# High and low tokens as one 512-column matmul in the feed-forward input projections and the second merge

## The chip, the cores and the metric

One NeuronCore of a Trainium2 chip runs the whole program. The metric is device time in microseconds, as the median of the runs; lower is better. Engines are called PE (TensorE, matmuls), ACT (ScalarE), DVE (VectorE), POOL (GpSimd) and SP (SyncE, which issues most of the transfers).

## What is computed

256 tokens with 2048 channels pass through four blocks of layers, all in float32. Two attention layers come first (one with a learned choice of keys), then a block with two mixers (sparse attention and a gated delta rule), whose outputs are merged by sigmoid gates, then a feed-forward part and a last norm. Cut to what the change touches, the reference is:

```
g_nsa, g_dn = split(sigmoid(merge_g), 2)          # merge_g: 4096 of the columns of h @ w_in
mixed = g_nsa * (o_nsa @ w_up_nsa) + g_dn * (o_dn @ w_up_dn)
x  = x + mixed @ w_o
h2 = rms_norm(x, norm2_w)
x  = x + (silu(h2 @ w_ffn_gate) * (h2 @ w_ffn_up)) @ w_ffn_down     # 2048 -> 5632 -> 2048
return rms_norm(x, norm_f_w)
```

## The kernel before

Every large product goes through one function, `gemm` (L121). Activations stay in SBUF, weights stream through once. To keep float32 precision with one-pass matmuls, both operands are split into a high part (the value rounded to the matmul's format) and a low part (the rest), and a product is the sum of three: high x high, high x low, low x high.

*Activations.* `new_T` (L206) makes a pair of tiles `hi` and `lo`, each [128 channels, 4 chunks, 256 tokens], for 512 channels. A product over 2048 channels takes a list of four such pairs, one over 1024 (`w_up_dn`) two. `to_T` and `x_T` (L211, L238) fill a pair from transposes on PE; ACT writes `hi`, DVE writes `lo`. The pairs have two tags of eight buffers, which other split tiles share (`slot`, L51).

*Weights.* For 512 input channels (loop `g`) SP loads a tile `raw` of 1 MB, [128, 4 chunks, 512 columns] (L134), into one of three buffers. Each half of it is cast on ACT to `wh` (L139) and subtracted on DVE to `wl` (L140); both have three buffers. A `wh`/`wl` pair of [128, 2, 512] so feeds two chunks.

*Matmuls.* `gemm` has two forms. In the token-major one (L152 to L157) the activations are loaded into the array and 512 columns of weights stream past them. In the channel-major one (`flip=True`, L145 to L150) 128 columns of weights are loaded and the 256 tokens stream past: first `hi` by `wh`, then `lo` by `wh`, then `hi` by `wl`, all added into one 256-column half of a PSUM bank. The result is 512 channels in two banks, and `evac(b, psum)` is called for both at the end. There are four banks for products (tag `mm`), so the next product fills the other two.

*Around the change.* In `second` (L1213 to L1302), after all mixers, a loop over four blocks of 512 channels computes the second merge: a gate product over 2048 channels (L1285, evacuated by `mgate`, L1264: DVE multiplies by the row of the norm's factors, ACT takes the tanh), then the product with `w_up_dn` (L1297), whose `evac` (L1287) multiplies by the gate, adds the first merge's block `md` and splits the sum into `mT`. Four token-major products with `w_o` follow (L1301); after each, one block of the new residual is normed and transposed into the list `h2`. In `ffn` (L1313) the 11 blocks of 512 hidden channels come in parts of 4, 4 and 3. For each block there is a gate product (L1329, `evac_g`: DVE multiplies by the row, ACT takes the silu) and an up product (L1338, `evac_u`: DVE multiplies by the row and by the gate, then the block is split). After each part the token-major products with `w_ffn_down` follow (L1348). Before the loop `row_of` (L166) turns the norm's factors into a row on all partitions by two small matmuls (L175) and a copy (L176).

*What sets the order.* Each engine runs its instructions in program order and waits on semaphores. The framework orders the traced instructions by a model of their times when the program is built, so the order on each engine is fixed before the run. Small background tasks are traced between the matmuls by `tick` (L92).

Of the kernel before, what the change touches and what calls it, by code (L numbers as in the profile page):

```python
# [11 lines left out]
F32 = mybir.dt.float32  # L12
# [14 lines left out]
class Kern:  # L27
    """The whole forward pass; activations stay in SBUF, weights stream through once."""

    def __init__(self, ctx, tc, d, out, stop=None):  # L30
# [9 lines left out]
        self.flip = False  # L40
        self.finished = set()

# [32 lines left out]
    def defer(self, n, fn):  # L75
        """trace fn after n further ticks"""
        self.later.append([n, fn])
# [14 lines left out]
    def tick(self):  # L92
        """advance deferred work and the background chains"""
# [27 lines left out]
    def gemm(self, xT, W, c0, n, evac, ng=4, split=False, flip=False):  # L121
# [3 lines left out]
        pt = [self.ps.tile([P, 512], F32, tag="mm", bufs=4, name="mm") for _ in range(2)]  # L125
        for g in range(ng):
# [8 lines left out]
            hi, lo = xT[g]  # L135
            for h in range(2):
                wh = self.sb.tile([P, 2, n], F32R, tag="wh", bufs=3, name="wh")
                wl = self.sb.tile([P, 2, n], F32R, tag="wl", bufs=3, name="wl")
                nc.scalar.copy(wh, raw[:, 2 * h:2 * h + 2])  # L139
                nc.vector.tensor_tensor(wl, raw[:, 2 * h:2 * h + 2], wh.bitcast(F32), ALU.subtract)  # L140
# [20 lines left out]

    @staticmethod
    def c2(ap):
        return ap.rearrange("p (c n) -> p c n", c=2)

    def row_of(self, r):  # L166
        """per-token columns r[t] [128, 1] -> [128, 2 (broadcast), 256 tokens] on every partition"""
# [11 lines left out]
    def gemm_by_tile(self, xT, W, c0, n, evac, ng):  # L179
        """a narrow gemm that keeps its split weights and ends one token tile before the other"""  # L180
        nc = self.nc
        ws = []
        for g in range(ng):
# [3 lines left out]
            for h in range(2):  # L187
# [4 lines left out]
                ws.append((wh, wl))  # L192
        for t in range(2):
            o = self.ps.tile([P, 512], F32, tag="mm", bufs=4, name="mm")[:, :n]
            ts = slice(t * P, (t + 1) * P)
            for g in range(ng):
                hi, lo = xT[g]
# [8 lines left out]
    def new_T(self):  # L206
        hi = self.sb.tile([P, 4, T], F32R, tag="hi", bufs=8, name="hi")
        lo = self.sb.tile([P, 4, T], F32R, tag="lo", bufs=8, name="lo")
        return hi, lo

    def to_T(self, src, gain=None, scale=None):  # L211
        """src(t, c): [128 tokens, 128 channels]; returns the split transpose of 4 chunks."""
        nc = self.nc
        hi, lo = self.new_T()
# [21 lines left out]
        return hi, lo  # L236
# [7 lines left out]
    def rsq(self, out, in_, mul, n, eps=EPS):  # L244
        """out = (in_ * mul + eps) ** -0.5"""
# [8 lines left out]
    def norm_rstd(self, ss, dst=None):  # L254
        """ss: per token tile [128, 4] block sums of squares -> (rstd, rstd / 2, rstd^2 / 128)"""
# [11 lines left out]
    def rope4(self, o, x, tC, tS, scal=None, heads=4, hd=128):  # L267
        """o = x * C + swap(x) * S over [128, heads, hd]; x in PSUM or SBUF; scal per partition."""
# [20 lines left out]
    def trans4(self, src, dst, scale=None, n=4, eng=None):  # L289
        """dst [128, n*128] = per-128-column-chunk transposes of src [128, n*128]."""  # L290
# [36 lines left out]
    def park_x(self):  # L327
        """the residual waits in DRAM while the mixers need its room"""
# [22 lines left out]
    def gains2(self):  # L351
        """per-channel columns of the second block: conv taps, position embeddings, norm gain"""
# [15 lines left out]
    def tables(self, rope, qn, kn, wait=0):  # L368
        """rope tables with a per-dimension gain folded in: [128, t, (C | S)]"""
# [28 lines left out]
    def attn_qprep(self, t, ps, tabs, r, r2, st):  # L398
        """raw q block of 4 heads in PSUM -> roped (gain in), transposed; st: scale per head."""
# [15 lines left out]
    def pipeline(self, units, stages):  # L415
        """software pipeline: one stage of each unit in flight per step"""
# [104 lines left out]
    def split_into(self, hi, lo, cs, a):  # L521
        """chunks cs of a split transpose from a [128, len(cs), 256]"""
# [3 lines left out]
    def residual_block(self, j, gain, ss, hT, last=False):  # L526
        """evacuation of block j of a projection onto the residual, then the next input's block"""
# [981 lines left out]
```

## Time and profile before

| | |
|---|---|
| runs | 2310.85, 2311.62, 2311.79 us; median 2311.62 |
| span of the profiled execution | 2308.8 us; the profile gives no other time of this execution |
| PE, loads of weights into PE | busy 2295.5 us (99%), 2094.7 us (91%) |
| DVE, ACT, POOL | busy 1395.8 us (60%), 1089.4 us (47%), 133.6 us (6%) |
| data moved by DMA | 404.70 MB, mean 175 GB/s |
| second merge ends, w_o ends | at about 1455 and 1547 us of the span; the feed-forward part follows |

The time of a run counts from the outside; the span is from the first to the last instruction of one execution under the profiler. Busy time is the union of an engine's instructions. Matmuls overlap on PE: a row's length is not the distance to the next start, and that distance has to be read from starts and counts. An idle time is put down to the instruction that released the semaphore.

### The profile page before, as it was taken

How to read it: one execution, taken by the hardware profiler on the slowest of the kernel's cores; microseconds unless marked ns; L12 is line 12 of the kernel's file. 1: busy time of each engine (PE TensorE's matmuls, PEld its weight loads, DVE VectorE, ACT ScalarE, POOL GpSimd, SP SyncE). 2: the span in 40 equal slices, each digit the busy share in tenths (PEclk: the TensorE clock that was granted, in tenths of full speed). 3: DMA queues.
4: the chain of work that ended last, by engine and by line, in shares of the span. 5: the costliest groups of instructions: out<-in, count | busy, mean ns of one | idle time of the engine just before them, and what ended most of it. 6: DMA issues, size and time to landing. Idle time of an engine off the chain costs nothing.

```text
span 2308.8 us, 39431 instructions
## 1 busy us (share of the span) xinstructions
PE 2295.5 (99%) x16446; PEld 2094.7 (91%) x16446; DVE 1395.8 (60%) x2073; ACT 1089.4 (47%) x1758; POOL 133.6 (6%) x233
## 2 busy tenths in 40 slices
PE   9999999999999999999999999999999999999998
PEld 8878998888998888999999999889998899989997
DVE  5686765656665656878675655555555455554555
ACT  5555644456544434564534444454443344433444
POOL 1011100112100300011101000000000000000000
PEclk9999999999999999999999999999999999999999
DMA  7544455654556754344443665555555555555554
GB/s 230 193 149 153 140 183 182 189 176 137 167 183 208 240 157 152 112 164 130 146 148 120 205 225 183 182 192 191 183 183 189 192 184 183 183 182 184 182 185 143
DMA packets 209811, 404.70 MB, mean 175 GB/s; under 512 B 7376, under 2 KB 25776, under 8 KB 209632
## 3 DMA queue, kind: packets, MB, share of 16 engines
q1 hardware_dynamic: 206880, 394.04, 52.5%
q0 software_dynamic: 2752, 8.13, 1.2%
q8 instruction: 129, 2.11, 0.4%
q14 instruction: 50, 0.41, 0.1%
HBM read 397.95 MB, written 4.19 MB: 174 GB/s over the span
## 4 chain that ended last, share of the span: by engine, by line
PE 99%; DMA 0%; DVE 0%; SPq 0%; ACT 0%; issue 0%; ACTq 0%; POOLq 0%; POOL 0%
PE mm L150 16%; PE mm L148 16%; PE mm L149 16%; PE mm L157 14%; PE mm L156 14%; PE mm L155 14%; PE lg L440 1%; PE tr L294 1%; PE tp L219 1%; PE hid L994 1%; PE nl L1086 0%; PE pt L473 0%; PE ib L638 0%; DMA x<-in_x_dram 0%; PE ov L490 0%; PE ov L491 0%
## 5 line engine op out<-in xcount | busy, mean ns | idle before, releaser
L140 DVE TENSOR_TENSOR wl<-raw,wh 128x1024 fp32r<-128x1024 f32 (+4 forms) x760 | 902.6, 1188 | 794.2 <-ACT wh L139 793.1
L139 ACT CAST wh<-raw 128x1024 fp32r<-128x1024 f32 (+4 forms) x760 | 775.9, 1021 | 1028.5 <-PE mm L149 550.3
L150 PE MATMUL mm<-hi,wl 128*128 128x256 f32 x3072 | 868.9, 284 | 0.0
L148 PE MATMUL mm<-hi,wh 128*128 128x256 f32 x3072 | 868.4, 283 | 0.0
L149 PE MATMUL mm<-lo,wh 128*128 128x256 f32 x3072 | 868.1, 283 | 0.0
L148 PEld LDWEIGHTS mm<-hi,wh 128*128 128x128 f32 x3072 | 579.8, 189 | 1.5 <-issue 0.5
L149 PEld LDWEIGHTS mm<-lo,wh 128*128 128x128 f32 x3072 | 579.2, 189 | 0.8 <-issue 0.2
L150 PEld LDWEIGHTS mm<-hi,wl 128*128 128x128 f32 x3072 | 577.9, 188 | 1.0 <-issue 0.2
L156 PE MATMUL mm<-wl,hi 128*128 128x512 f32 (+4 forms) x1504 | 574.6, 383 | 0.2 <-DVE wl L140 0.2
L157 PE MATMUL mm<-wh,lo 128*128 128x512 f32 (+4 forms) x1504 | 570.6, 381 | 0.0
L155 PE MATMUL mm<-wh,hi 128*128 128x512 f32 (+4 forms) x1504 | 529.3, 382 | 0.0
L156 PEld LDWEIGHTS mm<-wl,hi 128*128 128x128 f32 x1504 | 283.3, 188 | 55.4 <-issue 0.6
L157 PEld LDWEIGHTS mm<-wh,lo 128*128 128x128 f32 x1504 | 283.1, 188 | 55.0 <-issue 1.5
L155 PEld LDWEIGHTS mm<-wh,hi 128*128 128x128 f32 x1504 | 281.1, 189 | 56.2 <-issue 1.3
L248 POOL TENSOR_SCALAR rsqv<-nsum 128x1 f32<-128x1 f32 x10 | 3.5, 351 | 1228.4 <-DVE nsum L1361 744.4
L233 ACT ACTIVATE hi<-tp,gT 128x256 fp32r<-128x256 f32 x64 | 27.6, 471 | 21.3 <-PE tp L219 18.9
L454 ACT ACTIVATE lg<-lg,nb 128x128 f32<-128x128 f32 (+1 forms) x64 | 28.4, 445 | 16.7 <-POOL nb L447 16.7
L234 DVE SCALAR_TENSOR_TENSOR lo<-tp,gT,hi 128x256 fp32r<-128x256 f32 x64 | 28.4, 478 | 12.4 <-ACT hi L233 12.0
L730 DVE SCALAR_TENSOR_TENSOR cv<-raw,cols,cv 128x255 f32<-128x255 f32 (+2 forms) x72 | 31.1, 475 | 1.8 <-ACT cv L727 1.7
L252 ACT ACTIVATE junk<-x 128x512 bf16<-128x512 f32 (+1 forms) x42 | 25.6, 610 | 6.0 <-DMA x<-in_x_dram 2.2
L252 ACT ACTIVATE junk<-mm 128x128 bf16<-128x128 f32 x80 | 22.2, 278 | 7.3 <-PE mm L157 5.8
L440 PE MATMUL lg<-kT,qT 128*128 128x256 f32 (+1 forms) x128 | 23.7, 327 | 0.0
(378 smaller groups left out, 1386.2 us busy)
## 6 DMA issues: line engine op xcount, KB each, us to landing
raw<-in_w_in_dram SPq DMA_DIRECT2D x76, 1024.0 KB, 5.1
raw<-in_w_ffn_gate_dram SPq DMA_DIRECT2D x44, 1024.0 KB, 5.2
raw<-in_w_ffn_up_dram SPq DMA_DIRECT2D x44, 1024.0 KB, 5.2
raw<-in_w_ffn_down_dram SPq DMA_DIRECT2D x41, 1024.0 KB, 5.1
raw<-in_a_w_in_dram SPq DMA_DIRECT2D x40, 1024.0 KB, 5.1
raw<-in_b_w_in_dram SPq DMA_DIRECT2D x40, 1024.0 KB, 5.1
raw<-in_a_w_out_dram SPq DMA_DIRECT2D x16, 1024.0 KB, 5.0
raw<-in_b_w_out_dram SPq DMA_DIRECT2D x16, 1024.0 KB, 5.1
```

The source lines that it names most:

```text
L139: nc.scalar.copy(wh, raw[:, 2 * h:2 * h + 2])
L140: nc.vector.tensor_tensor(wl, raw[:, 2 * h:2 * h + 2], wh.bitcast(F32), ALU.subtract)
L148: nc.tensor.matmul(o, wh[:, c, ms], hi[:, kc], start=first and m % 2 == 0, stop=False)
L149: nc.tensor.matmul(o, wh[:, c, ms], lo[:, kc], start=False, stop=False)
L150: nc.tensor.matmul(o, wl[:, c, ms], hi[:, kc], start=False, stop=last and m % 2 == 1)
L155: nc.tensor.matmul(o, xh, wh[:, c], start=first, stop=False)
L156: nc.tensor.matmul(o, xh, wl[:, c], start=False, stop=False)
L157: nc.tensor.matmul(o, xl, wh[:, c], start=False, stop=last)
L234: nc.vector.scalar_tensor_tensor(lo[:, k], tp[:, c], g, hi[:, k].bitcast(F32), ALU.mult, ALU.subtract)
L252: self.nc.scalar.activation(self.junk()[:, :w], in_, AF.Square, accum_out=accum)
L440: nc.tensor.matmul(lb[:, i * S:(i + 1) * S], qT[:, h * P:(h + 1) * P], kT[:, :S], start=True, stop=True)
L730: v.scalar_tensor_tensor(o[:, s:], x[:, :T - s], self.convw[:, k:k + 1], o[:, s:], ALU.mult, ALU.add)
```

## The change

Two kinds of products get a function of their own, `gemm_T`: the gate and up products of the feed-forward part, and both products of the second merge. The first merge, the attention layers' gates and the delta rule's inputs keep `gemm` with `flip=True`.

In `gemm_T` the outer loop runs over two halves of 256 output channels. A half takes two banks, one for each 128 channels. `raw` is [128, 8 chunks, 256 columns]: 1 MB as before, over 1024 input channels, in rows of 1 KB. A `wh`/`wl` pair is [128, 4, 256] and feeds four chunks. For each chunk and each 128 channels there are two matmuls: `wh` with the 512 columns of high and low tokens side by side, into the whole bank, and `wl` with the 256 high ones into the bank's first half. The high and low tokens therefore share a tile, [128, 4, 2, 256], with one tag `hl` of eight buffers of double size. The evacuation runs after each half: `add_halves` copies the second half of a bank out on ACT and adds the first on DVE, and only then come the row and the rest; in `w_up_dn`'s evacuation the sum goes through a tile `halves` that has one buffer. Since the first `raw` covers 1024 channels, a product's start asks for two blocks of its input list.

The core of the diff:

```diff
     def slot(self, name, dt=F32):
-        self.flip = not self.flip
-        return self.sb.tile([P, 2, 512], dt, tag="hi" if self.flip else "lo", bufs=8, name=name)
+        if self.half is not None:
+            b, self.half = self.half, None
+        else:
+            t = self.sb.tile([P, 2, 2, 512], F32, tag="hl", bufs=8, name="half")
+            b, self.half = t[:, 0], t[:, 1]
+        return b if dt is F32 else b.bitcast(dt)
...
+    def weights(self, raw, h, n):
+        nc = self.nc
+        k = raw.shape[1] // 2
+        wh = self.sb.tile([P, k, n], F32R, tag="wh", bufs=3, name="wh")
+        wl = self.sb.tile([P, k, n], F32R, tag="wl", bufs=3, name="wl")
+        nc.scalar.copy(wh, raw[:, k * h:k * h + k])
+        nc.vector.tensor_tensor(wl, raw[:, k * h:k * h + k], wh.bitcast(F32), ALU.subtract)
+        return wh, wl
...
+    def gemm_T(self, xT, W, c0, evac, ng=4):
+        nc = self.nc
+        for b in range(2):
+            pt = self.banks()
+            for g2 in range(ng // 2):
+                self.flush(lambda: len(xT) > 2 * g2 + 1 and None not in xT[2 * g2:2 * g2 + 2])
+                raw = self.sb.tile([P, 8, T], F32, tag="raw", bufs=3, name="raw")
+                nc.sync.dma_start(raw, W[g2 * 1024:(g2 + 1) * 1024,
+                                         c0 + b * T:c0 + (b + 1) * T].rearrange("(c p) n -> p c n", p=P))
+                for h in range(2):
+                    wh, wl = self.weights(raw, h, T)
+                    hl = xT[2 * g2 + h][2]
+                    for c in range(4):
+                        first = g2 == 0 and h == 0 and c == 0
+                        last = g2 == ng // 2 - 1 and h == 1 and c == 3
+                        for m in range(2):
+                            ms = slice(m * P, (m + 1) * P)
+                            nc.tensor.matmul(self.c2(pt[m]), wh[:, c, ms], hl[:, c],
+                                             start=first, stop=False)
+                            nc.tensor.matmul(pt[m][:, :T], wl[:, c, ms], hl[:, c, 0],
+                                             start=False, stop=last)
+                        if c % 2:
+                            self.tick()
+            evac(b, pt)
...
+    def add_halves(self, o, bank):
+        self.nc.scalar.copy(o, bank[:, T:])
+        self.nc.vector.tensor_tensor(o, bank[:, :T], o, ALU.add)
+
+    def joined(self, o, pt, row):
+        for i in range(2):
+            self.add_halves(o[:, i], pt[i])
+        self.nc.vector.tensor_tensor(o, o, row, ALU.mult)
...
     def new_T(self):
-        hi = self.sb.tile([P, 4, T], F32R, tag="hi", bufs=8, name="hi")
-        lo = self.sb.tile([P, 4, T], F32R, tag="lo", bufs=8, name="lo")
-        return hi, lo
+        hl = self.sb.tile([P, 4, 2, T], F32R, tag="hl", bufs=8, name="hl")
+        return hl[:, :, 0], hl[:, :, 1], hl
...
-            self.gemm(hT, W, 6696 + 2048 + 512 * j, 512, lambda b, ps: mgate(m[b], ps), flip=True)
+            self.gemm_T(hT, W, 6696 + 2048 + 512 * j, lambda b, pt: mgate_T(m[b], pt))
...
-                v.scalar_tensor_tensor(m[b], m[b], 1.0, ps, ALU.add, ALU.mult)
+                for i in range(2):
+                    up, mi = self.halves(), m[b][:, i]
+                    self.add_halves(up, pt[i])
+                    v.scalar_tensor_tensor(mi, mi, 1.0, up, ALU.add, ALU.mult)
...
-            self.gemm(dT, d["w_up_dn_2"][0], 512 * j, 512, evac, ng=2, flip=True)
+            self.gemm_T(dT, d["w_up_dn_2"][0], 512 * j, evac, ng=2)
...
-                    v.tensor_tensor(s[b], ps, row, ALU.mult)
+                    self.joined(s[b], pt, row)
...
-                self.gemm(h2, d["w_ffn_gate_2"][0], 512 * jb, 512, evac_g, flip=True)
+                self.gemm_T(h2, d["w_ffn_gate_2"][0], 512 * jb, evac_g)
...
-                self.gemm(h2, d["w_ffn_up_2"][0], 512 * jb, 512, evac_u, flip=True)
+                self.gemm_T(h2, d["w_ffn_up_2"][0], 512 * jb, evac_u)
```

Two places show how the instructions are laid out now. The first is PE where one product of the feed-forward part ends and the next begins; `mm` is a bank, `hi`, `lo` and `hl` are split activations, and the number after a name tells buffers apart. Before:

```order
L148 MATMUL mm_16376<-hi_15603,wh_16407 128x256
L149 MATMUL mm_16376<-lo_15604,wh_16407 128x256
L150 MATMUL mm_16376<-hi_15603,wl_16408 128x256
L148 MATMUL mm_16375<-hi_15767,wh_16437 128x256
L149 MATMUL mm_16375<-lo_15768,wh_16437 128x256
L150 MATMUL mm_16375<-hi_15767,wl_16438 128x256
```

With the change, where a half of a product ends and the next begins:

```order
L196 MATMUL mm_15892<-hl_15804,wh_15957 128x512
L198 MATMUL mm_15892<-hl_15804,wl_15958 128x256
L196 MATMUL mm_15984<-hl_15271,wh_15988 128x512
L196 MATMUL mm_15985<-hl_15271,wh_15988 128x512
L198 MATMUL mm_15984<-hl_15271,wl_15989 128x256
L198 MATMUL mm_15985<-hl_15271,wl_15989 128x256
```

Three narrow matmuls have become a wide and a narrow one (L196 and L198 are the two lines of `gemm_T`); at the start of a half the two wide ones come first.

The second place is ACT from the start of the feed-forward part to the first gate block's silu: `hi` or `hl` from `tp` are the last block of h2, `sg` is the gate. Before:

```order
L139 CAST wh<-raw 128x1024 x2
L233 ACTIVATE hi<-tp,gT 128x256 x4
L139 CAST wh<-raw 128x1024
L176 COPY row<-row 128x256
L139 CAST wh<-raw 128x1024 x5
L1328 ACT_TABLE_LOAD
L1328 ACTIVATE sg_16113<-sg_16113 128x512
L1328 ACTIVATE sg_16114<-sg_16114 128x512
```

With the change, to the silu of the first half:

```order
L135 CAST wh<-raw 128x1024 x2
L290 ACTIVATE hl<-tp,gT 128x256 x3
L135 CAST wh<-raw 128x1024
L290 ACTIVATE hl<-tp,gT 128x256
L135 CAST wh<-raw 128x1024
L232 COPY row<-row 128x256
L213 COPY sg_15778<-mm 128x256
L135 CAST wh<-raw 128x1024
L213 COPY sg_15778<-mm 128x256
L135 CAST wh<-raw 128x1024 x2
L1392 ACT_TABLE_LOAD
L1392 ACTIVATE sg_15778<-sg_15778 128x512
```

The last quarter of h2 now stands behind a weight cast. The half's evacuation puts two copies ahead of the silu, with a weight cast between them.

## Rows read from the trace of the kernel before

**Rows 1.** Page: span; busy us, share of the span and instructions of each engine.

```profile
span 2308.8 us, 39431 instructions
...
PE 2295.5 (99%) x16446; PEld 2094.7 (91%) x16446; DVE 1395.8 (60%) x2073; ACT 1089.4 (47%) x1758; POOL 133.6 (6%) x233
```

**Rows 2.** Page: chain that ended last, by engine and by line.

```profile
PE 99%; DMA 0%; DVE 0%; SPq 0%; ACT 0%; issue 0%; ACTq 0%; POOLq 0%; POOL 0%
PE mm L150 16%; PE mm L148 16%; PE mm L149 16%; PE mm L157 14%; PE mm L156 14%; PE mm L155 14%; PE lg L440 1%; PE tr L294 1%; PE tp L219 1%; PE hid L994 1%; PE nl L1086 0%; PE pt L473 0%; PE ib L638 0%; DMA x<-in_x_dram 0%; PE ov L490 0%; PE ov L491 0%
```

**Rows 3.** PE's waits, whole span: us in total, times, longest us; first and last.

```profile
PE warm L311 <- DVE zero L308: 1.7, 1, 1.7
...
PE mm L156 <- DVE wl L140: 0.2, 1, 0.2
```

**Rows 4.** Stretches of PE: us, busy (instructions), granted clock, DMA share, GB/s.

```profile
1300.00:1450.00 150.00, 150.00 (x1266) 1.00 0.59 197
1565.00:1725.00 160.00, 160.00 (x1350) 1.00 0.57 185
1825.00:2000.00 175.00, 175.00 (x1461) 1.00 0.56 181
2100.00:2230.00 130.00, 130.00 (x1086) 1.00 0.57 185
1735.00:1815.00 80.00, 80.00 (x346) 1.00 0.55 184
2010.00:2090.00 80.00, 80.00 (x345) 1.00 0.56 185
```

**Rows 5.** Groups by shape: busy us, mean ns of one | idle before; matmuls.

```profile
L150 PE MATMUL mm<-hi,wl 128*128 128x256 f32 x3072 | 868.9, 284 | 0.0
...
L156 PE MATMUL mm<-wl,hi 128*128 128x512 f32 x1256 | 499.3, 398 | 0.0
```

**Rows 6.** Groups by shape: evacuations and weight splits.

```profile
L140 DVE TENSOR_TENSOR wl<-raw,wh 128x1024 fp32r<-128x1024 f32 x698 | 853.8, 1223 | 741.7 <-ACT wh L139 741.0 <-issue 0.2
L139 ACT CAST wh<-raw 128x1024 fp32r<-128x1024 f32 x698 | 732.6, 1050 | 957.2 <-PE mm L149 544.2 <-PE mm L157 393.9 <-issue 11.1
...
L234 DVE SCALAR_TENSOR_TENSOR lo<-tp,gT,hi 128x256 fp32r<-128x256 f32 x64 | 28.4, 478 | 12.4 <-ACT hi L233 12.0
...
L283 DVE TENSOR_TENSOR rope<-mm,tabs 128x256 f32<-128x256 f32 x40 | 15.0, 413 | 0.0
...
L1336 DVE TENSOR_TENSOR up<-up,sg 128x512 f32<-128x512 f32 x22 | 14.1, 683 | 0.0
...
L493 ACT COPY o<-ov 128x256 f32<-128x256 f32 x32 | 11.1, 374 | 13.9 <-PE ov L491 13.6
```

**Rows 7.** Waits, whole span: ACT's casts for PE.

```profile
ACT wh L139 <- PE mm L149: 550.3, 341, 5.0
```

**Rows 8.** DMA, 1830:1900: packets, MB, share of engines; issues, us to landing.

```profile
q1 hardware_dynamic: 6341, 12.59, 55.9%
...
raw<-in_w_ffn_up_dram SPq DMA_DIRECT2D x7, 1024.0 KB, 5.2
```

**Rows 9.** DMA, 2270:2283: the same columns.

```profile
q1 hardware_dynamic: 1202, 1.20, 29.6%
...
raw<-in_w_ffn_down_dram SPq DMA_DIRECT2D x3, 512.0 KB, 3.4
```

**Rows 10.** Timeline, start of the feed-forward: start us, us, instruction.

```profile
1553.88 1.04 PE L219 MATMUL tp<-ident,x 128*128 128x128 f32 x8
...
1555.37 1.50 DVE L234 SCALAR_TENSOR_TENSOR lo<-tp,gT,hi 128x256 fp32r<-128x256 f32 x3
...
1556.99 0.48 DVE L234 SCALAR_TENSOR_TENSOR lo<-tp,gT,hi 128x256 fp32r<-128x256 f32 x1
```

**Rows 11.** Timeline of PE in the first attention layer: start us, us, instruction.

```profile
193.86 0.40 PE L491 MATMUL ov<-pT,vl 128*128 128x512 f32 x1
194.09 0.40 PE L156 MATMUL mm<-wl,hi 128*128 128x512 f32 x1
```

More of the change, by code (lines that the diff above doesn't have):

```diff
@@ L39, in __init__ @@
         self.later = []
-        self.flip = False
+        self.half = None
         self.finished = set()
@@ L118, in ready, with banks @@
             yield
+    def banks(self):
+        return [self.ps.tile([P, 512], F32, tag="mm", bufs=4, name="mm") for _ in range(2)]
+    def weights(self, raw, h, n):
[6 more added lines that the diff above has]
+        return wh, wl
     def gemm(self, xT, W, c0, n, evac, ng=4, split=False, flip=False):
         nc = self.nc
-        pt = [self.ps.tile([P, 512], F32, tag="mm", bufs=4, name="mm") for _ in range(2)]
+        pt = self.banks()
         for g in range(ng):
@@ L134, in gemm @@
                 nc.sync.dma_start(raw, src)
-            hi, lo = xT[g]
+            hi, lo, _ = xT[g]
             for h in range(2):
[L137 to L140, printed above, removed]
+                wh, wl = self.weights(raw, h, n)
                 for c in range(2):
@@ L160, in gemm @@
             evac(t, self.c2(pt[t]) if flip else pt[t][:, :n])
+    def gemm_T(self, xT, W, c0, evac, ng=4):
+        nc = self.nc
+        for b in range(2):
+            pt = self.banks()
+            for g2 in range(ng // 2):
[18 more added lines that the diff above has]
+            evac(b, pt)
     @staticmethod
@@ L164, in c2, with halves @@
         return ap.rearrange("p (c n) -> p c n", c=2)
+    def halves(self):
+        return self.sb.tile([P, T], F32, tag="halves", bufs=1, name="halves")
+    def add_halves(self, o, bank):
[5 more added lines that the diff above has]
+        self.nc.vector.tensor_tensor(o, o, row, ALU.mult)
     def row_of(self, r):
@@ L192, in gemm_by_tile @@
                 ws.append((wh, wl))
+        pt = self.banks()
         for t in range(2):
-            o = self.ps.tile([P, 512], F32, tag="mm", bufs=4, name="mm")[:, :n]
+            o = pt[t][:, :n]
             ts = slice(t * P, (t + 1) * P)
             for g in range(ng):
-                hi, lo = xT[g]
+                hi, lo, _ = xT[g]
                 for c in range(4):
@@ L235, in to_T @@
                                                    ALU.mult, ALU.subtract)
-        return hi, lo
+        return hi, lo, hl
     def x_T(self, j, gain):
@@ L576, in evac @@
                 nc.vector.tensor_tensor(th, th, o[b], ALU.mult)
-                self.split_into(*oT[-1], slice(2 * b, 2 * b + 2), th)
+                self.split_into(*oT[-1][:2], slice(2 * b, 2 * b + 2), th)
             self.gemm(hT, w_in, cg + 512 * g, 512, evac, flip=True)
@@ L1148, in values @@
                 b = o[t].rearrange("p (h q) -> p h q", h=4)
-                hi, lo = (x[:, :, t * P:(t + 1) * P] for x in dst)
+                hi, lo = (x[:, :, t * P:(t + 1) * P] for x in dst[:2])
                 nc.scalar.copy(hi, b)
@@ L1266, in mgate, with mgate_T @@
             nc.scalar.activation(m, m, AF.Tanh)
+        def mgate_T(m, pt):
+            self.joined(m, pt, rowh)
+            nc.scalar.activation(m, m, AF.Tanh)
         for j in range(4):
@@ L1324, in ffn, with evac_g, evac_u @@
                 s = [self.c2(self.w2(f"sg{b}")) for b in range(2)]
-                def evac_g(b, ps):
-                    v.tensor_tensor(s[b], ps, row, ALU.mult)
+                def evac_g(b, pt):
+                    self.joined(s[b], pt, row)
                     nc.scalar.activation(s[b], s[b], AF.Silu)
-                self.gemm(h2, d["w_ffn_gate_2"][0], 512 * jb, 512, evac_g, flip=True)
-                hi, lo = self.new_T()
-                aT.append((hi, lo))
-                def evac_u(b, ps):
+                self.gemm_T(h2, d["w_ffn_gate_2"][0], 512 * jb, evac_g)
+                aT.append(self.new_T())
+                hi, lo, _ = aT[-1]
+                def evac_u(b, pt):
                     u = self.c2(self.w2("up"))
-                    v.tensor_tensor(u, ps, row, ALU.mult)
+                    self.joined(u, pt, row)
                     v.tensor_tensor(u, u, s[b], ALU.mult)
                     self.split_into(hi, lo, slice(2 * b, 2 * b + 2), u)
-                self.gemm(h2, d["w_ffn_up_2"][0], 512 * jb, 512, evac_u, flip=True)
+                self.gemm_T(h2, d["w_ffn_up_2"][0], 512 * jb, evac_u)
             Wd = d["w_ffn_down_2"][0, p0 * 512:p1 * 512]
```

6 lines of the change are left out of this document (3 added, 3 removed).

## The prediction

> **What bounds the kernel now.** I read the share of each engine first, then the chain that ended last, then TensorE's waits. PE is busy for 99% of a span of 2308.8 us, VectorE (DVE) for 60% and ScalarE (ACT) for 47% [rows 1]. The chain that ended last is 99% PE, and nearly all of it is six lines: the three matmuls of the channel-major products (L148 to L150, 16% each) and the three of the token-major ones (L155 to L157, 14% each) [rows 2]. PE's own waits in the whole program are a few microseconds, the longest 1.7 us, all but 0.2 us of it before the first product [rows 3]. So PE never starves: in the stages that the change touches, time is the number of matmuls times the distance from one start to the next. Work on another engine or a transfer counts only if it makes PE wait.
>
> That distance can't be read from the mean of a group, since successive matmuls overlap (a 256-column row lasts 284 ns [rows 5]). I take it from stretches inside one stage, as length by count; the count holds some matmuls that were already running at the left edge (284 or 398 ns by the distance: 2.4 of the narrow, 1.7 of the wide), which I take off. The 256-column matmuls of the merge: 150 us by 1263.6 is **118.7 ns**; of the first feed-forward part 160 by 1347.6, 118.7; of the second 175 by 1458.6 and of the third 130 by 1083.6, **120.0**. The 512-column matmuls of the down projections: 80 by 344.3 is **232.4 ns**, and 80 by 343.3 is **233.0** [rows 4]. The granted clock is 1.00 throughout, that is 2.4 GHz, at which 256 columns are 106.7 ns and 512 are 213.3. So a narrow matmul carries 12.0 to 13.3 ns beyond its columns and a wide one 19.1 to 19.7: less than two narrow ones carry together.
>
> **The change, part by part.** *Matmuls.* For 128 output channels and one chunk of 128 inputs, three 256-column matmuls become one of 512 (wh times high and low) and one of 256 (wl times high). The columns are the same, 768. A gate, up or second-merge gate product has 16 chunks x 4 groups of channels = 64 such pairs, a w_up_dn product 32. Feed-forward: 22 products, 1408 pairs; second merge: 4 x 64 + 4 x 32 = 384. In all 1792 pairs: PE's program loses 3584 narrow matmuls and gains 1792 wide ones, and is the same up to the first block of the second merge.
>
> Each pair trades two narrow distances for a wide one. I take the wide distance from the down projections, whose place in the program is nearest. Merge and first part, 896 pairs: 2 x 118.7 - 232.4 = 5.0 ns, 4.5 us. Second and third part, 896 pairs: 2 x 120.0 - 233.0 = 7.0 ns, 6.3 us. Sum **10.8 us**. Ends from the same rows: 2 x 118.7 - 233.0 = 4.4 ns gives 7.9 us, 2 x 120.0 - 232.4 = 7.6 ns gives 13.6 us. The weight loads go with their matmuls; they lie under the matmul before and set no distance here.
>
> The Trainium skill, TensorE: Matmul & The Clock Gate, section Back-to-back issue gap, puts a warm matmul at its columns by 2.4 GHz plus 2.5 ns. By that the change would save 2.5 ns a pair, 4.5 us, and end near 2307. This trace does not agree: 12 to 20 ns stand there instead of 2.5.
>
> *Evacuation.* High and low products now lie in two halves of a bank and must be added. Per half block (256 channels) that adds two ACT copies of 256 out of PSUM (nearest row 374 ns) and two DVE adds (413 ns); the multiplication by the row stays, at 683 ns [rows 6]. There are 60 half blocks (44 in the feed-forward, 16 in the merge): 45 us of ACT and 50 us of DVE. I cost them at nothing, because PE waits for them only through two things. The banks: a half block has two of the four and they are wanted again a half block later, at 32 x 351 ns = 11.2 us (5.6 for w_up_dn). And the split weights: a wh/wl pair feeds 8 pairs of matmuls, 2.8 us, and there are three. ACT already waits for PE to free one, 550 us in 341 waits on L149 alone [rows 7], so the ring is full and two tiles are ready when a third is freed. After a half block's end ACT has a copy, then the cast (1.05 us), DVE the split (1.22): 2.65 us, against 5.6 until PE wants that tile. If this cover of 3.0 us went, PE would wait.
>
> The tightest place is w_up_dn. There DVE has two adds, two multiply-adds of 256 (478 ns), an add and a split of 512 (683 each) and two weight splits: 5.6 us of work in a half block of 5.6, in turns with ACT through one scratch tile. It falls behind by a microsecond or so and catches up in the next gate block, where DVE has 8 x 1.22 + 2 x 1.5 = 12.8 us in 22.5. I take no wait there, with up to 2 us per product (8 in all) as the other end.
>
> *Transfers.* A weight tile is still 1 MB, in rows of 1 KB instead of 2 KB. The page has such rows in the last blocks of the down projection: 1.20 MB took 29.6% of 13 us on all DMA engines, 312 GB/s at full use, against 12.59 MB in 55.9% of 70 us, 322, for 2 KB rows; half a megabyte landed in 3.4 us, a whole one of 2 KB rows in 5.2 [rows 8, 9]. So the share rises from 0.56 to about 0.60, and a tile lands in 5.2 to 6.8 us (twice 3.4) where two tiles' use, 11.2 us, lies between the freeing of a slot and the need. Nothing.
>
> *Start of the feed-forward.* The last block of h2 is transposed while the first gate product runs. Before, 53 matmuls stand ahead of the transposes and the block is wanted at the 145th, 91 x 119 ns = 10.8 us later. Now 42 stand ahead and it is wanted at the 49th: 6 matmuls, 1.05 us, after the transposes. Before, the transposes began at 1553.88 and took 1.04 us, and the last of the four splits ended at 1557.47, 3.6 us after their begin [rows 10]. The first quarter was then ready about 2.0 us after that begin, and is now wanted at 1.04 + 1.05 = 2.1; the last quarter is wanted 6 pairs later, at 4.2, with a weight cast and split (2.3 us on two engines) now ahead of it. I take **0.5 us** of waiting, between 0 and 2.
>
> Sum: 10.8 - 0.5 = 10.3 us off. The profiled execution gives its span alone, 2308.8 us; the median of the runs, 2311.6, is 2.8 longer, around the span, where the change adds and removes nothing. Span 2298.5, time **2301.3**.
>
> **The rivals.** *More is saved* (0.11). The 19 ns of a wide matmul may belong to the token-major form, where fresh weights are streamed, and a merged one carry only a narrow one's 12.7. Then a pair saves 12.7 ns, 22.8 us: 2289. Against it: the attention's wide matmuls, which also stream split activations past loaded values, start 0.23 us before their followers [rows 11], as the down projections do.
>
> *Little is saved* (0.14). What a matmul carries may go mostly with its columns. Two narrow ones carry 24 to 26.6 ns; a merged one that carries as much, at 237 to 240, saves nothing, and halfway 5 us: 2307 to 2312, about 2310. For it: only two widths are compared above, and they stand in products of different form. The Trainium skill's rule above would end at this rival's lower edge.
>
> *Slower* (0.08). The place is the end of each of the 60 half blocks. ACT's program has the copy that waits for PE's last matmul ahead of the next cast. Were only one weight tile ready there instead of two, both copies, the cast and the split would take 3.0 to 3.4 us against 2.8, and PE would wait 0.2 to 0.6 us at each end: 12 to 36 us, middling 24, and 2325. It decides from 0.18 us an end on, where the saving is used up. For it: ACT's order now alternates copies and casts. Against: the waits of ACT for PE, which say that the ring is full.
>
> That the change doesn't do what it says (0.01): the order shows that it does.
>
> **How the numbers follow.** My forecast has 0.66 and by itself spans 2297 to 2306 (13.6 saved, none lost; 7.9 saved, 2 lost). The range goes down to 2294, part of the way to the first rival, and up to 2308, into the second; it leaves out about 2 in 10. About 0.2%, 4.6 us, is what a measurement here can tell from no change: 2307.0 to 2316.2. Faster: 0.66 + 0.11 + 0.03 of the second rival, 0.80. Same: the rest of it and the idle change, 0.12. Slower: 0.08.
>
> **What would show it.** Right: 1792 wide matmuls in the touched lines, narrow ones at 118 to 120 and wide ones at 231 to 234 ns from start to start, a pair near 351; PE's waits still a few microseconds, most of the new ones near the feed-forward's start; ACT and DVE busier by some 45 and 50 us; DMA share near 0.60. Wrong: a pair at 344 or at 356 and more; or waits of PE for wl or wh after each half block's end.

## The result and the profile after

The changed kernel takes **2297.37 us** (median of 4 runs, 2297.12 to 2298.25); the kernel before, run beside it on the same chip, 2311.65. The ratio is 0.994, with a 95% interval of 0.9926 to 0.9954: 14.3 us off, where 10.3 were forecast. The time lies inside the range, 3.9 us below the point.

The page and TensorE's waits, as in [rows 1 to 3]:

```profile
span 2296.5 us, 36096 instructions
...
PE 2282.1 (99%) x14654; PEld 2004.2 (87%) x14654; DVE 1447.3 (63%) x2201; ACT 1123.4 (49%) x1878; POOL 133.5 (6%) x233
...
PE 99%; DMA 0%; DVE 0%; SPq 0%; ACT 0%; issue 0%; ACTq 0%; POOLq 0%; POOL 0%
PE mm L196 18%; PE mm L172 14%; PE mm L171 14%; PE mm L170 14%; PE mm L198 9%; PE mm L165 7%; PE mm L163 7%; PE mm L164 7%; PE lg L497 1%; PE tr L351 1%; PE tp L276 1%; PE hid L1051 1%; PE nl L1143 0%; PE pt L530 0%; PE ib L695 0%; DMA x<-i
```

```profile
PE tp L276 <- DMA x<-in_x_dram: 3.8, 1, 3.8
PE warm L368 <- DVE zero L365: 1.7, 1, 1.7
PE mm L171 <- DVE wl L136: 0.2, 1, 0.2
```

PE lost 1792 matmuls and is still all of the chain. L196 is the merged matmul, L198 the narrow one that stays, L163 to L165 the channel-major products that were left alone, L170 to L172 the token-major ones. None of PE's waits stands in a changed stage. DVE gained 51.5 us and ACT 34 (45 was forecast for it), and PE waits for neither.

Where the time went is read from stretches cut at the first matmul of each stage: second merge, `w_o`, first part's gates and ups, its down projection, second part, its down projection, third part, the rest. (The last starts with the third down projection.) Columns: stretch, its length, busy us (instructions) of PE, PEld (weight loads), DVE, ACT and POOL, the granted clock, DMA share, GB/s. The kernel before:

```profile
1318.64:1455.35 136.71, 136.71 (x1155) 136.71 (x1153) 76.19 (x77) 58.14 (x62) 0.00 (x0) 1.00 0.60 201
1455.35:1547.37 92.02, 92.02 (x410) 74.64 (x409) 51.14 (x57) 43.43 (x58) 0.00 (x0) 1.00 0.55 183
1547.37:1730.97 183.60, 183.60 (x1549) 183.60 (x1548) 98.06 (x101) 79.73 (x88) 5.34 (x12) 1.00 0.59 190
1730.97:1820.19 89.22, 89.22 (x387) 72.36 (x385) 46.15 (x45) 34.81 (x34) 0.00 (x0) 1.00 0.57 189
1820.19:2004.51 184.32, 184.32 (x1538) 184.32 (x1537) 96.04 (x93) 75.07 (x78) 0.00 (x0) 1.00 0.57 183
2004.51:2094.10 89.59, 89.59 (x386) 72.10 (x385) 46.17 (x45) 34.80 (x34) 0.00 (x0) 1.00 0.56 188
2094.10:2232.34 138.24, 138.24 (x1154) 138.24 (x1152) 71.49 (x69) 55.97 (x58) 0.00 (x0) 1.00 0.57 183
2232.34:2308.80 76.46, 67.33 (x362) 57.64 (x360) 42.93 (x62) 33.65 (x54) 1.50 (x4) 0.97 0.46 152
```

The changed kernel:

```profile
1320.14:1454.87 134.73, 134.73 (x771) 118.03 (x769) 91.39 (x116) 67.92 (x94) 0.00 (x0) 1.00 0.65 203
1454.87:1546.79 91.92, 91.92 (x410) 74.69 (x409) 51.20 (x58) 43.24 (x59) 0.00 (x0) 1.00 0.55 183
1546.79:1727.69 180.90, 180.90 (x1037) 158.62 (x1036) 111.73 (x133) 88.75 (x120) 5.25 (x12) 1.00 0.59 192
1727.69:1816.92 89.23, 89.23 (x386) 72.37 (x385) 45.73 (x44) 34.60 (x35) 0.00 (x0) 1.00 0.57 189
1816.92:1996.52 179.60, 179.60 (x1025) 157.30 (x1024) 109.53 (x125) 84.17 (x110) 0.00 (x0) 1.00 0.58 188
1996.52:2085.75 89.23, 89.23 (x387) 72.36 (x385) 45.73 (x44) 34.61 (x35) 0.00 (x0) 1.00 0.57 189
2085.75:2220.45 134.70, 134.70 (x770) 118.02 (x769) 81.72 (x93) 62.85 (x82) 0.00 (x0) 1.00 0.59 188
2220.45:2296.50 76.05, 67.34 (x362) 57.64 (x360) 42.41 (x61) 33.41 (x55) 1.50 (x4) 0.98 0.46 153
```

Line by line the changes are -1.98, -0.10, -2.70, +0.01, -4.72, -0.36, -3.54 and -0.41: **13.8 us** from the second merge to the end. The profiled execution began its work 1.5 us later (it waited 3.8 us for its input, the one before 1.3 and 1.0), so the spans differ by only 12.3; this start moves from one execution to the next, and is no part of the change.

Two things are to be seen here. A group of three narrow matmuls, 360.0 ns in the second part before (184.32 us by 512), became a group of two in 350.8 (179.60 by 512), and the third part gives the same. And the column PEld: before, weight loads fill the whole of every narrow stretch, 183.60 of 183.60 us and so on; after, 87 to 88% of it. I had read only that they lie beside the matmuls. By itself, though, the column doesn't say that loads set the distance: a load's row lasts 0.19 us (188 to 192 ns), so loads that start less than 0.19 us apart fill it, whatever keeps them apart.

### The profile page after: what moved, and what is told of

Same layout as the page of the kernel before. It is cut to its first block, busy times and chain, and to the rows that moved or that the text cites. A ratio compares the mean times of both kernels' runs of the same rounds, so it can differ in the third digit from the quotient of the medians.

```text
span 2296.5 us, 36096 instructions
## 1 busy us (share of the span) xinstructions
PE 2282.1 (99%) x14654; PEld 2004.2 (87%) x14654; DVE 1447.3 (63%) x2201; ACT 1123.4 (49%) x1878; POOL 133.5 (6%) x233
## 4 chain that ended last, share of the span: by engine, by line
PE 99%; DMA 0%; DVE 0%; SPq 0%; ACT 0%; issue 0%; ACTq 0%; POOLq 0%; POOL 0%
PE mm L196 18%; PE mm L172 14%; PE mm L171 14%; PE mm L170 14%; PE mm L198 9%; PE mm L165 7%; PE mm L163 7%; PE mm L164 7%; PE lg L497 1%; PE tr L351 1%; PE tp L276 1%; PE hid L1051 1%; PE nl L1143 0%; PE pt L530 0%; PE ib L695 0%; DMA x<-in_x_dram 0%
## 5 line engine op out<-in xcount | busy, mean ns | idle before, releaser
L135 ACT CAST wh<-raw 128x1024 fp32r<-128x1024 f32 (+4 forms) x760 | 776.4, 1022 | 897.7 <-PE mm L172 450.7
L196 PE MATMUL mm<-hl,wh 128*128 128x512 f32 x1792 | 622.7, 394 | 0.0
L171 PE MATMUL mm<-wl,hl 128*128 128x512 f32 (+4 forms) x1504 | 574.6, 383 | 0.2 <-DVE wl L136 0.2
L172 PE MATMUL mm<-wh,hl 128*128 128x512 f32 (+4 forms) x1504 | 570.8, 382 | 0.0
L170 PE MATMUL mm<-wh,hl 128*128 128x512 f32 (+4 forms) x1504 | 529.2, 382 | 0.0
L198 PE MATMUL mm<-hl,wl 128*128 128x256 f32 x1792 | 491.9, 282 | 0.0
L196 PEld LDWEIGHTS mm<-hl,wh 128*128 128x128 f32 x1792 | 330.9, 188 | 70.3
L163 PE MATMUL mm<-hl,wh 128*128 128x256 f32 x1280 | 362.6, 284 | 0.0
L164 PE MATMUL mm<-hl,wh 128*128 128x256 f32 x1280 | 362.3, 283 | 0.0
L165 PE MATMUL mm<-hl,wl 128*128 128x256 f32 x1280 | 361.7, 284 | 0.0
L198 PEld LDWEIGHTS mm<-hl,wl 128*128 128x128 f32 x1792 | 336.8, 188 | 7.6
L171 PEld LDWEIGHTS mm<-wl,hl 128*128 128x128 f32 x1504 | 283.6, 189 | 55.1 <-issue 0.6
L172 PEld LDWEIGHTS mm<-wh,hl 128*128 128x128 f32 x1504 | 283.4, 189 | 55.0 <-issue 1.5
L170 PEld LDWEIGHTS mm<-wh,hl 128*128 128x128 f32 x1504 | 281.4, 189 | 56.1 <-issue 1.3
L163 PEld LDWEIGHTS mm<-hl,wh 128*128 128x128 f32 x1280 | 241.1, 188 | 1.3 <-issue 0.5
L164 PEld LDWEIGHTS mm<-hl,wh 128*128 128x128 f32 x1280 | 241.1, 188 | 0.7 <-issue 0.2
L165 PEld LDWEIGHTS mm<-hl,wl 128*128 128x128 f32 x1280 | 240.3, 188 | 1.0 <-issue 0.2
L291 DVE SCALAR_TENSOR_TENSOR hl<-tp,gT,hl 128x256 fp32r<-128x256 f32 x64 | 28.5, 478 | 13.3 <-ACT hl L290 13.2
```

Source lines behind the costliest of these rows:

```text
L135: nc.scalar.copy(wh, raw[:, k * h:k * h + k])
L163: nc.tensor.matmul(o, wh[:, c, ms], hi[:, kc], start=first and m % 2 == 0, stop=False)
L164: nc.tensor.matmul(o, wh[:, c, ms], lo[:, kc], start=False, stop=False)
L165: nc.tensor.matmul(o, wl[:, c, ms], hi[:, kc], start=False, stop=last and m % 2 == 1)
L170: nc.tensor.matmul(o, xh, wh[:, c], start=first, stop=False)
L171: nc.tensor.matmul(o, xh, wl[:, c], start=False, stop=False)
```

## The experiments

**The matmuls alone.** `unmerge` keeps everything of the change but the merged matmul:

```diff
-nc.tensor.matmul(self.c2(pt[m]), wh[:, c, ms], hl[:, c], start=first, stop=False)
+nc.tensor.matmul(pt[m][:, :T], wh[:, c, ms], hl[:, c, 0], start=first, stop=False)
+nc.tensor.matmul(pt[m][:, T:], wh[:, c, ms], hl[:, c, 1], start=False, stop=False)
```

> Everything of the change stays (half blocks, 1 KB rows, shared tiles, evacuation), but the 512-column matmul is two of 256 again, with the same weights: 1792 matmuls more. Theory of a fixed part per matmul: three narrow ones take 356 to 360 ns where the pair took 351, so 9 to 16 us more than the changed kernel, 2306 to 2313 us, about the kernel before. Rival, the gain came from the new layout or order and not from the width: 2302 us or less.

Measured: 2311.12 us, ratio 1.0 (0.9992 to 1.0009). Its first part, second part, down projection and third part:

```profile
1547.07:1730.68 183.61, 183.61 (x1550) 183.60 (x1549) 111.64 (x133) 88.90 (x120) 5.33 (x12) 1.00 0.59 190
1819.89:2004.21 184.32, 184.32 (x1538) 184.32 (x1536) 109.59 (x125) 84.09 (x110) 0.00 (x0) 1.00 0.56 183
2004.21:2093.80 89.59, 89.59 (x386) 72.07 (x385) 45.73 (x44) 34.56 (x35) 0.00 (x0) 1.00 0.57 188
2093.80:2232.04 138.24, 138.24 (x1153) 138.23 (x1152) 81.74 (x93) 62.89 (x82) 0.00 (x0) 1.00 0.56 183
```

The lengths of before are back to 0.01 us, with the DVE and ACT work of after. The whole gain is the merged matmul's; half blocks, shared tiles, 1 KB rows and evacuation neither cost nor give.

**The evacuation.** `lite` drops the copy and the addition (shown where the row multiplies; likewise in the evacuation of w_up_dn):

```diff
-for i in range(2):
-    self.add_halves(o[:, i], pt[i])
-self.nc.vector.tensor_tensor(o, o, row, ALU.mult)
+for i in range(2):
+    self.nc.vector.tensor_tensor(o[:, i], pt[i][:, :T], row[:, 0], ALU.mult)
```

> The changed kernel, but the evacuation leaves out the low half: VectorE takes only the first 256 columns of each bank, with no copy by ScalarE and no addition, so the result lacks the terms with the low tokens. It takes away the some 95 us of work that the change added on ScalarE and VectorE. Theory (all of it is hidden, the matmuls alone bound these stages): 2297.4 us, 2296.7 to 2298.1. Rival (a part of the added evacuation shows at the half blocks' ends): 60 half blocks by 0.1 to 0.5 us, so 2267 to 2291 us.

Measured: 2297.85 us (2297.47 to 2298.17). Its second part takes as long as after's, with 10 us less DVE work:

```profile
1815.99:1995.68 179.69, 179.69 (x1025) 157.50 (x1024) 99.58 (x111) 75.82 (x79) 0.00 (x0) 1.00 0.58 188
```

All of the added evacuation is hidden. What hides it is shown by `whole`, which does a product's 512 channels at once, in all four banks, again with rows of 2 KB:

```diff
-for b in range(2):
-    pt = self.banks()
-    for g2 in range(ng // 2):
+pt = self.banks() + self.banks()
+for g in range(ng):
...
+for b in range(2):
+    evac(b, pt[2 * b:2 * b + 2])
```

> The changed kernel with each product done at once for all 512 output columns: four banks fill together and are emptied at the end, and the weights come in rows of 2 KB as in the kernel before. The matmuls are the same. Theory (two banks fill while two are emptied, which is why the evacuation costs nothing): the next product now waits for the four copies and additions before it, 1 to 1.3 us at each of 30 products, so 2325 to 2338 us, and the trace shows these waits on the additions. Rival (the evacuation is short enough not to need the second pair of banks, and longer rows help): 2294 to 2299 us.

Measured: 2309.43 us, 12.1 more than the change; 27 to 40 were expected, and the rival had none. So the direction held and the price was a third, about 0.4 us a product: by stage 5.3 us over the merge's 8 products and 6.3 over the 22 of the feed-forward, 0.7 and 0.3 each. The waits of PE's weight loads in `whole` (in after none of these is found; a load's wait is lost time only as far as no matmul streams meanwhile):

```profile
PEld mm L195 <- DVE wl L136: 10.1, 29, 0.4
...
PEld mm L193 <- DVE halves L211: 2.3, 3, 0.8
PEld mm L193 <- DVE sg L211: 2.1, 11, 0.2
...
PEld mm L193 <- DVE up L211: 1.5, 8, 0.2
```

The timeline around one such product of the feed-forward (start us, us, engine, instruction, the idle time before):

```profile
1845.41 1.07 ACT L210 COPY sg<-mm 128x256 f32<-128x256 f32 x3 [0.83 <-PE mm L195]
...
1845.82 1.12 DVE L211 TENSOR_TENSOR sg<-mm,sg 128x256 f32<-128x256 f32 x3
...
1846.14 0.28 PE L195 MATMUL mm<-hl,wl 128*128 128x256 f32 x1
1846.29 0.19 PEld L193 LDWEIGHTS mm<-hl,wh 128*128 128x128 f32 x1 [0.19 <-DVE sg L211]
...
1846.38 1.05 ACT L135 CAST wh<-raw 128x1024 fp32r<-128x1024 f32 x1
```

In the feed-forward the additions (L211) hold a bank for only 0.2 us; those of w_up_dn, through the one tile `halves`, hold it up to 0.8. The most waiting, 10.1 us, comes from what stands behind them: ACT's cast (L135) starts after the copies, DVE's subtraction after the additions, and the weight loads of a later chunk wait for `wl` 29 times, which is the queueing that my rival "slower" described. I had priced the wait for the banks and missed that. Two banks filling while two are emptied are worth 12 us here, if the longer rows that came with `whole` are worth nothing, as `unmerge` says of the shorter ones.

**What a matmul carries.** `dose` cuts the narrow matmul that stays into two of 128 columns, on the same weights:

```diff
-nc.tensor.matmul(pt[m][:, :T], wl[:, c, ms], hl[:, c, 0], start=False, stop=last)
+nc.tensor.matmul(pt[m][:, :P], wl[:, c, ms], hl[:, c, 0, :P], start=False, stop=False)
+nc.tensor.matmul(pt[m][:, P:T], wl[:, c, ms], hl[:, c, 0, P:], start=False, stop=last)
```

> The changed kernel, with the 256-column matmul of wl cut into two of 128 columns: 1792 matmuls more, the same columns. Theory of a fixed part of about 5 to 7 ns: 9 to 13 us more, 2306 to 2311 us. Rival, a matmul can't start sooner after the last than its own weights take, and 128 columns are too short to cover that: more than 20 us more, over 2317 us. Rival, what a matmul carries goes with its columns: 2298 us.

Measured: 2481.33 us, ratio 1.0736: far outside the theory's range, and as the first rival, the weights' own load, had it. The second part:

```profile
1908.98:2141.03 232.05, 232.05 (x1537) 210.45 (x1536) 110.19 (x125) 83.51 (x110) 0.00 (x0) 1.00 0.45 146
```

A group takes 453.2 ns (232.05 us by 512). With a wide one at 232.4, half the columns still cost 110.4 ns each, against about 119 for all 256. A saving per matmul counted in a fixed number of nanoseconds can't be right at this width. The timeline shows what is kept apart (start us, us, engine, instruction):

```profile
1950.01 0.22 PE L198 MATMUL mm<-hl,wl 128*128 128x128 f32 x1
1950.01 0.19 PEld L200 LDWEIGHTS mm<-hl,wl 128*128 128x128 f32 x1
1950.07 0.27 PE L200 MATMUL mm<-hl,wl 128*128 128x128 f32 x1
1950.12 0.19 PEld L196 LDWEIGHTS mm<-hl,wh 128*128 128x128 f32 x1
1950.18 0.45 PE L196 MATMUL mm<-hl,wh 128*128 128x512 f32 x1
1950.23 0.19 PEld L198 LDWEIGHTS mm<-hl,wl 128*128 128x128 f32 x1
```

The loads start 0.11 us apart. The two matmuls of 128 columns, each on a load of its own, start only 0.06 apart. So 0.11 us is a distance between loads, and not a floor for any two matmuls.

Two runs change columns alone. `cols192` starts from `unmerge`, `wide384` from the change (of the three matmuls of `cols192` one is shown):

```diff
+w = T if first else 192
-nc.tensor.matmul(pt[m][:, :T], wh[:, c, ms], hl[:, c, 0], start=first, stop=False)
+nc.tensor.matmul(pt[m][:, :w], wh[:, c, ms], hl[:, c, 0, :w], start=first, stop=False)
...
-nc.tensor.matmul(self.c2(pt[m]), wh[:, c, ms], hl[:, c], start=first, stop=False)
+nc.tensor.matmul(self.c2(pt[m])[:, :, :w], wh[:, c, ms], hl[:, c, :, :w], start=first, stop=False)
```

> The kernel with the matmuls cut again (three of 256 columns to a group), but in all chunks after a block's first, 1672 groups, each of the three matmuls takes only 192 of its 256 columns: the last 64 tokens are left out of the product there. Asked is what a narrow matmul's distance of 118.6 to 120 ns consists of. Theory A (columns, and some 12 ns on top): 64 columns are 26.7 ns at 2.4 GHz, so 5016 x 26.7 = 134 us less than 2311.1, 2177 us, and the distance is 92 ns. Theory B (the weight load sets it, as the run with 128 columns and TensorE's load row, busy for the whole of these stages, suggest): the distance stays between 110 and 120 ns, 2270 to 2311 us; on a line from 110.5 ns at 128 columns to 118.6 at 256 it is 114.5, 2290 us.

> The changed kernel, but in all chunks after a block's first, 1672 groups, the merged matmul takes 192 columns of the high and 192 of the low tokens, 384 in place of 512: the last 64 tokens are left out of these products. Asked is what the merged matmul's 232.4 ns consist of. Columns and 19 ns on top: 128 columns are 53.3 ns at 2.4 GHz, so 1672 x 53.3 = 89 us less than 2297.4, 2208 us, and a group of 297.7 ns. What stands on top of the columns shrinks with them (15.5 ns instead of 19): 294 ns, 2202 us. Something of fixed length beneath (two weight loads and a wait for each other): the group stays near 351 ns, 2290 to 2297 us.

Measured: 2272.06 us and 2201.96 us. The second part of `cols192`:

```profile
1803.19:1975.40 172.21, 172.21 (x1537) 172.20 (x1536) 109.57 (x125) 84.06 (x110) 0.00 (x0) 1.00 0.61 196
```

and of `wide384`:

```profile
1768.28:1920.48 152.20, 152.20 (x1025) 150.75 (x1024) 109.50 (x125) 84.11 (x110) 0.00 (x0) 1.00 0.68 221
```

`cols192`: 112.1 ns a matmul, 111.6 for the short ones when the sixteenth that is still at full width is put at 120. By columns 92 were expected: theory A falls. B's range holds, at its lower end; its line had given 114.5 ns and 2290 us. Together: 128 columns take 110.4 ns, 192 take 111.6, 256 take 118.7 to 120.0. Between 128 and 192 columns the columns hardly matter: a matmul on a new weight block of 128 x 128 costs at least about **110 ns**. That this is the load is read from the starts in `dose`; in the timeline of `cols192` the loads start 0.11 us apart as well. The Trainium skill, TensorE: Matmul & The Clock Gate, section LDWEIGHTS, puts the load of 128 weight columns at 128 / 1.2, that is 106.7 ns; these runs agree within 5%.

`wide384`: a group of 297.3 ns, 293.7 for the short ones when the sixteenth at 350.8 is taken out. Less a narrow matmul at 118.6 that is 175.1 ns for 384 columns (the starts in the trace give 175.3 and 118.7 on average), 57.3 less than for 512. So a wide one costs about **0.45 ns a column** (0.456 at 384, 0.454 at 512) where 2.4 GHz gives 0.417, and, on the line through the two, only 3 ns fixed (232.4 less 512 x 57.3 / 128). The expectation "shrinks with them" gave 294 ns and 2202 us and was met. The load row is nearly full here too (150.75 of 152.20 us), in a run whose wide matmuls go by their columns: a full row doesn't show that loads are the limit.

**The steady distances.** Before, the second and third parts stood at 120.0 ns, merge and first part at 118.7, with the same instructions. `nudge1` puts one small matmul ahead of the second part of the kernel before (in the profile it stands at 1735.4 us, early in the down projection in between, and not late as expected):

```diff
+if p0 == 4:
+    nb = self.bank("nudge")
+    nc.tensor.matmul(nb[:, :16], self.ones, self.ident[:, :16], start=True, stop=True)
```

> The kernel before with one small matmul more, late in the first down projections, ahead of the second feed-forward part, where narrow matmuls stood 120.0 ns apart. If the narrow stream has several steady rhythms and the way it is entered selects one, the distance in the second part changes (118.7 or 122) and the time moves by 2 to 3 us. Rival, the distance belongs to the place (buffers, data): it stays 120.0 and the time stays within 0.5 us.

Measured: 2311.84 us in a single run, and the second part as before, 184.32 us:

```profile
1821.56:2005.88 184.32, 184.32 (x1537) 184.31 (x1536) 96.07 (x93) 75.06 (x78) 0.00 (x0) 1.00 0.56 183
```

`only2` takes the change and cuts its matmul again everywhere but in the second part:

```diff
+if self.cut:        # self.cut = p0 != 4 in ffn, True in the merge
+    nc.tensor.matmul(pt[m][:, :T], wh[:, c, ms], hl[:, c, 0], start=first, stop=False)
+    nc.tensor.matmul(pt[m][:, T:], wh[:, c, ms], hl[:, c, 1], start=False, stop=False)
+else:
     nc.tensor.matmul(self.c2(pt[m]), wh[:, c, ms], hl[:, c], start=first, stop=False)
```

> The changed kernel, with the 512-column matmul cut in two again in the merge and in the first and the third part of the feed-forward; only the second part keeps it. Asked is whether the steady distance between matmuls is passed on from the stage ahead or belongs to the place in the program. Passed on: the second part runs at 351.0 ns for a group, its down projection at 232.4, and the third part's triples at 118.7 ns per matmul (356), so 2311.1 - 4.7 - 1.7 = 2304.7 us. By the place: the third part's triples stand at 120.0 ns (360), the down projection at 232.4 or 233.4, and the time is 2311.1 - 4.7 = 2306.4 us, less 0.3 where the down projection moves. The theory of 5 ns for a pair at every place gives 2311.1 - 2.6 = 2308.5 us.

Measured: 2306.24 us. Second part, its down projection, third part:

```profile
1821.47:2001.07 179.60, 179.60 (x1025) 157.34 (x1024) 109.58 (x125) 84.15 (x110) 0.00 (x0) 1.00 0.58 188
2001.07:2090.30 89.23, 89.23 (x386) 72.37 (x385) 45.74 (x44) 34.60 (x35) 0.00 (x0) 1.00 0.56 189
2090.30:2228.54 138.24, 138.24 (x1154) 138.24 (x1152) 81.74 (x93) 62.90 (x82) 0.00 (x0) 1.00 0.57 183
```

"By the place" gave 2306.4, less 0.3. The merged second part saves its 4.72 us alone, the down projection behind it goes to 232.4 ns a matmul, and the narrow third part is back at 120.0 although the stage ahead of it now runs as behind the first part. What in the place makes 118.7 or 120.0 stays open.

**Further in the same direction.** `extend` gives `gemm_T` to all other channel-major products: the attention layers' gates, the delta rule's inputs and the first merge, 1280 groups.

```diff
-self.gemm(hT, w_in, cg + 512 * g, 512, evac, flip=True)
+self.gemm_T(hT, w_in, cg + 512 * g, evac)
```

> The remaining channel-major products (attention gates, inputs of the delta rule, first merge: 1280 triples) get the same form. Theory of a fixed part: pairs at 351 ns there too, against 356 ns where the narrow ones run at 118.7 and 366 where they run at 122: 6.4 to 19 us less than the changed kernel, 2278 to 2291 us. Rival, the added evacuations and the background work of these stages make PE wait: 2295 us or more, with new PE waits in the profile.

Measured: 2295.90 us, only 1.5 less than the change: outside the theory's range and as the rival had it. The first attention layer's gates are the main reason. The theory's upper end was also wrong: in the traces the narrow matmuls of these stages start 118.4 to 119.1 ns apart on average, and none stand at 122, so about 6 us were to be had. Their stretch after, and in `extend`:

```profile
224.82:330.25 105.43, 105.43 (x875) 104.69 (x874) 72.70 (x117) 58.54 (x113) 6.67 (x12) 1.00 0.50 160
```

```profile
224.62:332.59 107.97, 105.41 (x623) 92.38 (x622) 80.03 (x134) 62.42 (x131) 5.75 (x12) 1.00 0.50 156
```

Now PE is not busy throughout. The chain of waits of `extend` there (start us, us, what):

```profile
...
259.94 0.60 DVE lg L520
260.55 1.13 DVE wl L136
261.76 0.33 DVE gt L214
262.13 0.51 PE mm L196
```

The bank's addition (`gt`, L214) stands on DVE behind the attention's softmax (`lg`) and a weight split, and PE's next block waits for it. The second layer's gates gained 1.4 us (101.54 to 100.11 by the same view). `extend_b` leaves the first layer's gates as they were:

```diff
+if paired:          # paired = mask != "dsa": the second attention layer
     self.gemm_T(hT, w_in, cg + 512 * g, evac)
+else:
+    self.gemm(hT, w_in, cg + 512 * g, 512, evac, flip=True)
```

> The extended kernel, with the first attention layer's gates as they were in the kernel before (four products, 256 triples, three matmuls each). In the extended kernel that layer's gates took 2.3 us longer than in the changed kernel although its merged products were 1.0 us shorter, and its waits of TensorE for the evacuation and for the attention's half tiles add up to 3.5 us. Theory (the evacuation by halves is late only there, where the attention's softmax runs beside it): the time falls by 2.3 us against the extended kernel, to 2293.6 us, 2293 to 2294.2, and no wait on an addition of halves is left. Rival (the waits are a share of every product that stands beside background work, and move elsewhere): 2295.5 to 2297 us.

Measured: **2292.15 us** (2291.89 to 2292.79), ratio 0.9916 (0.9901 to 0.993): the fastest kernel here that computes the whole result, 5.2 us below the change and below the expected range. The gates' stretch is at 105.43 us again, 2.54 less, about as expected. The medians differ by 3.75 us, the profiled spans by 3.2, of which 0.8 is the start (the first wait for the input is 3.0 us instead of 3.8); the rest is not explained. One thing expected did not come: a wait on an addition is left, 1.2 us in the delta rule's inputs.

## Why the prediction came out as it did

*The bound.* Right. PE stayed at 99% and sets the time; the time that the change took off is count times distance.

*Merge and first part, 5.0 ns by 896 groups.* Right: 4.5 us forecast, 1.98 + 2.70 = 4.7 measured.

*Second and third part, 7.0 ns by 896.* This step was mis-sized: 6.3 us forecast, 4.72 + 3.54 = 8.3 measured, 9.2 ns a group. It took the narrow matmul that stays at 120.0 and the wide one at 233.0, the distances of those stages before. With the merge a group takes 350.8 ns in all three parts, the sum of the quick pair 118.6 and 232.4. The narrow stages alone stood at the slower distance, as `unmerge` and `only2` show.

*The down projection behind the second part* gained 0.36 us, which I had not counted; in `only2` it does so when only the stage ahead is merged. So, of the 3.5 us between the 10.3 forecast and the 13.8 in the stages, 2.2 are the distances in the groups, 0.4 this stage and 0.5 the wait at the start of the feed-forward, which did not come; 0.5 lie in stages that the change doesn't touch.

*Evacuation and transfers at nothing.* Right, shown by `unmerge` and `lite`; w_up_dn's blocks too, since the merge saved in full. DMA's share in the parts is 0.58 to 0.59, in the merge 0.65 against 0.60.

*Start of the feed-forward, 0.5 us of waiting.* None came: TensorE's waits after list none there. The first part is 1.30 us longer than the second and holds eight transposes, which the timeline after shows at

```profile
1554.38 1.04 PE L276 MATMUL tp<-ident,x 128*128 128x128 f32 x8
```

and the two matmuls of the row.

*The reason.* Here the forecast was right for a number and not for what lies under it. I divided a distance into columns and 12 to 19 ns beyond them, and wrote that the weight loads set no distance. `cols192` and `dose` show that a narrow matmul stands just above its weight load, 118.7 ns against 110 to 112: the sentence on the loads holds at 256 columns by 7 to 9 ns, and fails at 192 and 128. `wide384` shows that a wide one pays by the column, with hardly anything fixed. That is why so little is saved. The line through 384 and 512 columns gives 117.8 ns at 256, so that both widths pay nearly by the column, and by that line a merge saves only the fixed 3 ns. Two narrow ones cost 237 to 240 ns against 232.4; the 2 to 4 ns beyond the 3 are not explained. The forecast got them because it took measured distances, without knowing what they consist of. The second rival's mechanism, that the excess goes with the columns, is largely true; its price was not. The first rival, a fixed excess of 12.7 ns, is excluded by the group of 350.8.

A row that shows the load was there in the trace of the kernel before: 16 matmuls of 16 columns (in plain float32), on blocks of 128 x 128, take 1.70 us to the next start, about 106 ns each, near the 110 found here:

```profile
893.43 1.85 PE L1055 MATMUL cl<-kc,q2T 128*128 128x16 f32 x16
895.13 0.48 PE L157 MATMUL mm<-wh,lo 128*128 128x512 f32 x1
```

The Trainium skill, Perfetto Trace Analysis, section Identifying the Most-Contended Engine, asks for the busy share of LDWEIGHTS, together with the share of the peak rate, in place of the busy share of matmuls. In this case the busy share of loads doesn't decide by itself: the load row is full in the narrow stages, in `cols192` and nearly in `wide384`, and it takes the starts of the loads to tell these apart.

## What to carry to other kernels

Before merging narrow matmuls, read from the timeline how far apart the weight loads start in that stage, and price a matmul at the larger of its load and its columns: here 110 ns against 0.45 ns a column and some 3 ns. From these runs I estimate that merging two of 128 columns would save 102 ns (2 x 110.4 - 118.7); merging two of 256 saved 5 to 9. And look at what the new form's evacuation queues behind: it was free where two banks fill while two are emptied and DVE is busy for some 60% of the stage, and cost more than the merge gave beside the attention's softmax.

## What was not expected of the hardware

The same stream of narrow matmuls stands at 118.7 ns in two stages and at 120.0 in two others, to 0.1 ns in every kernel here that keeps it, with the granted clock at 1.00 in all; the narrow stages that the change left alone start 118.4 to 119.1 ns apart on average, so that the second and third part are the exception; one more matmul, 86 us ahead, or a merged stage ahead does not move it, while a token-major stage goes between 232.4 and 233.3 with the stage ahead. It is worth 1.5 us in the third part, and its cause is open. That a matmul with half the columns costs 110.4 ns instead of 118.7, so that cutting 1792 narrow ones in two added 184 us, is the plainest sight of that floor in these traces.
